# Beginning layer two's feed-forward with the first token tile while the second tile's residual is summed

## The chip, the cores and the metric

The kernel runs on one core of one Trainium2 chip. The metric is the device time of one execution in microseconds (us), the median of several runs. The engines are named as in the profile: PE (TensorE, matmul), DVE (VectorE), ACT (ScalarE), POOL (GpSimd), SP (SyncE, here only a queue of DMAs). "ps" tiles lie in PSUM, all others on chip in SBUF.

## The reference, cut to what matters

Two decoder layers on 256 tokens of width 2048 (two token tiles of 128). What the change touches is the seam between the second layer's output projection and its gated MLP:

```python
def _finish_layer(x, heads, w_o, norms, w_up, w_conv, b_conv, w_down):
    x = x + _rmsnorm(heads @ w_o, norms[1])
    f = _conv_ffn(_rmsnorm(x, norms[2]), w_up, w_conv, b_conv, w_down)
    return x + _rmsnorm(f, norms[3])

def _conv_ffn(h, w_up, w_conv, b_conv, w_down):
    u = h @ w_up
    gate, val = jnp.split(u, 2, axis=-1)
    ...
    return (jax.nn.silu(acc) * val) @ w_down
```

## The kernel before, in words

All products are made of float32 values split in two parts, a rounded high part (written by ACT) and the rest as a low part (written by DVE): high x high, low x high and high x low make three matmuls (`mm3`). Every weight goes by DMA into a `raw` tile (3 buffers) and is split into a `w` tile (4 buffers) by `split` (lines 699 and 700): a cast on ACT, a subtraction on DVE.

`out_proj` multiplies the attention heads by `wo_b` in four chunks of 512 columns. The last two pieces of the last chunk ("late") are held split in a tile of their own (`stores`), so that all products of token tile 0 come first and then those of tile 1. `evac` squares a finished bank with an accumulated sum (`square_into`, L270, ACT), makes the reciprocal root mean square (`rstd`: a sum on DVE, L262, a power on POOL, L264) and multiplies by the gain (L616, DVE). `add_normed` (L599, DVE) adds four chunks of 512 columns to the residual `x[:, t]`. For layer two the first tile's residual is summed while PE multiplies the second tile's products; the second's follows, and with each chunk of it `x_T` is called.

`x_T` turns the residual: PE transposes (L306) 128x128 blocks of both token tiles into a PSUM bank that holds two blocks of 256 columns. `scaled_T` scales each block by the norm's gain and splits it into `h`: high part by ACT (L294), low part by DVE (L295), each from the same bank. PSUM has two sets of four banks, tags "g" and "s".

`ffn` multiplies h by the up weights, first eight narrow tiles of 128 output columns (`narrow(0)`, `ws_pair`, `ws_tile`: 16 depth blocks `kt` of two matmuls each, L173, one of 512 columns and one of 256), and then in the wide phases (`wide`) by 512 columns at a time with seven products for every unit u of two depth blocks, the first three of them plain: product 1 and 2 with the first token tile's h. `first_sums` and `sums_of_h` prepare sums of weights and of h for the other four. `rms` (ACT squares of x, L270) gives the norm's factor, which is applied later.

What sets the order: the program is written for a scheduler that lays out each engine's queue from priorities, tile buffers and dependencies; instructions that pass through `pin` while `self.pinned` is set keep the order in which they are written. `later` and `step` put a piece of work behind a number of weight tiles. The scheduler also adds all waits on semaphores; two engines that read one PSUM bank are made to wait for each other.

Of the kernel before, what the change touches and what calls it, by code (L numbers as in the profile page):

```python
# [10 lines left out]
F32 = mybir.dt.float32  # L11
# [38 lines left out]
class Body:  # L50
# [59 lines left out]
    def piece(self, src, cuts=1, store=None, between=None):  # L110
# [13 lines left out]
        for h in range(2):  # L124
            if store:
                hi, lo = (v[:, h * 1024:(h + 1) * 1024] for v in store)
            else:
                hi, lo = self.halves()
# [28 lines left out]
    def ws_tile(self, out, src, h, fresh=False):  # L157


        b = self.bank()  # L160
        self.step()
        raw = self.sb.tile([P, 2048], F32, name="raw", tag="raw", bufs=3)
        self.nc.sync.dma_start(raw, src)
        parts = [self.ws_parts(raw, i, FAR if fresh else APART, fresh) for i in range(2)]
# [51 lines left out]
    def as_mm(self, banks, parts, lhs, pi, tiles=(0, 1), cols=slice(0, 512)):  # L216
# [7 lines left out]
        for k, t in order:  # L224
# [4 lines left out]
            self.mm3(banks[t][:, cols], hi[:, ts], lo[:, ts], whi[:, ks], wlo[:, ks], kt == 0, kt == n - 1)  # L229

# [14 lines left out]
    def stores(self, which):  # L245

        w = self.sb.tile([P, 4, 2048], F32R, name=which, tag=which, bufs=1)
        return [(w[:, 2 * i, :], w[:, 2 * i + 1, :]) for i in range(2)]
# [9 lines left out]
    def rstd(self, ss):  # L258
# [3 lines left out]
        nc.vector.reduce_sum(v, ss, axis=AX.X)  # L262
# [5 lines left out]
    def square_into(self, src, acc):  # L268
        junk = self.sb.tile([P, 512], BF16, name="junk", tag="junk", bufs=1)
        return self.nc.scalar.activation(junk[:, :src.shape[-1]], src, AF.Square, scale=float(D) ** -0.5, accum_out=acc)  # L270
# [18 lines left out]
    def scaled_T(self, src, kt, g, h):  # L289
# [4 lines left out]
        self.last_hi = nc.scalar.activation(hi[:, kt, :], src, AF.Copy, scale=gc)  # L294
        nc.vector.scalar_tensor_tensor(lo[:, kt, :], src, gc, hi[:, kt, :].bitcast(F32),  # L295
                                       op0=ALU.mult, op1=ALU.subtract)
# [296 lines left out]
    def add_normed(self, ys, r, t, each=None):  # L593

        for c in range(4):
            if each and c:
                each(c - 1)
            xs = self.x[:, t, c * 512:(c + 1) * 512]
            self.nc.vector.scalar_tensor_tensor(xs, ys[c][:, t, :], r, xs, op0=ALU.mult, op1=ALU.add)  # L599
# [3 lines left out]
    def out_proj(self, layer, src, lhs, each, filler=None):  # L603
# [3 lines left out]
        for c0 in (0, 2):  # L607
# [3 lines left out]
            def evac(i, t):  # L611
# [4 lines left out]
                nc.vector.tensor_tensor(ys[c][:, t, :], banks[i][t], gs[i], op=ALU.mult)  # L616
# [15 lines left out]
            if late:  # L632

                store = self.stores("h2")
                parts = [self.piece(src[c0 + i][pi], store=st) for (i, pi), st in zip(late, store)]
                for t in range(2):
                    for (i, pi), p in zip(late, parts):
                        self.as_mm(banks[i], p, lhs, pi, (t,))
                    evac(late[-1][0], t)
        if filler:  # L640
            self.later(3, lambda: self.add_normed(ys, r[1], 1, each))
            filler()
        else:
            self.add_normed(ys, r[1], 1, each)
# [66 lines left out]
    def wide(self, src, then, ahead, h, s, forms, r, beside, also, outs=None):  # L711
# [10 lines left out]
        ps = {i: self.bank("g" if i in (1, 2, 6, 7) else "s") for i in range(1, 8)}  # L722
# [12 lines left out]
        def copied(u):  # L735

            c = self.near[:, 16 + u % 2 * P:][:, :P]
            pin(nc.scalar.copy(c, lhs(1, u)[0]))
            return c

        def load(u):

            raw = self.sb.tile([P, 2048], F32, name="raw", tag="raw", bufs=3)
            pin(nc.sync.dma_start(raw[:, :1536], src[u][:, :1536]))
# [9 lines left out]
        def plain(raw):  # L754
            fa, fb = self.halves(), self.halves()
            self.split(*fa, raw[:, 0:1024])
# [21 lines left out]
        f, first = plain(raw), copied(0)  # L778
        self.pinned = True
        for u in range(n):  # L780
# [6 lines left out]
            product(1, u, fa, 1, first)  # L787
            product(2, u, fa, 0)
            product(3, u, fb, 0)
# [4 lines left out]
            if more:  # L794
                raw = load(u + 1)
                after = beside[u + 1]()
                t, f = sums(ahead.pop(0), raw), plain(raw)
# [42 lines left out]
    def ffn(self, layer, h, each, filler=None, done=None, late=None):  # L840
# [108 lines left out]
        def narrow(g):  # L949
            for p in (2 * g, 2 * g + 1):  # L950
# [3 lines left out]
                ga = self.ws_pair(up[w, 0], h)  # L954
# [56 lines left out]
        for g in WIDE:  # L1011
            phase = WIDE.index(g)
            then = uw[phase + 1] if g < WIDE[-1] else None
            made = self.wide(uw[phase], then, ahead, h, s, forms, R[0], beside(g + 1), rest if phase == 0 else {})
# [73 lines left out]
    def run(self):  # L1088
# [245 lines left out]
        hh, hl, _ = self.hset("h1")  # L1334
        heads[2] = (hh[:, 0:4, :], hl[:, 0:4, :])
        lhs = [(mh[:, i, :], ml[:, i, :]) for i in range(4)] + [outs(i) for i in range(12)]
        box = []

        def each(c):
            if not box:  # L1340
                box.append(self.hset("h2"))
            self.x_T(COL_G["b2"], box[0], [c])

        self.out_proj(1, a["wo_b"], lhs, each)
        h = box[0]

        def store(t, c):
# [3 lines left out]
        self.ffn(1, h, None, done=store)  # L1351
# [99 lines left out]
```

## Time and profile before

| | us |
|---|---|
| time, median of 3 runs | 2140.63 (2140.34 to 2140.84) |
| the profiled execution | 2141.77 |
| its span | 2139.9 |
| PE busy | 2126.7 (99%) |
| DVE busy | 1737.7 (81%) |
| ACT busy | 1360.5 (64%) |
| granted clock of PE | 0.999 |

The span reaches from the first to the last instruction; busy times leave out waits. In rows of the timeline the columns are start, duration, engine, line and operation, output and input, and a count where equal instructions follow each other without a break; in square brackets stands the idle time before the row and who ended it. L-numbers are lines of the kernel before.

### The profile page before, as it was taken

What the parts mean: (1) busy time and instruction counts of PE and PEld (TensorE: products, weight loads), DVE (VectorE), ACT (ScalarE), POOL (GpSimd) and SP (SyncE); (2) the same over time, 40 slices, a digit from 0 to 9 for tenths busy, and PEclk for the clock granted to TensorE, in tenths of its full rate; (3) what the DMA queues carried; (4) which work ended last, traced back from release to release, by engine and by line L of the source; (5) the groups of instructions that cost most, each with busy time, mean ns of one, the idle gap of its engine ahead of it and who ended that gap; (6) DMA issues with size and microseconds to landing.
All of it is one profiled execution on the core that took longest, in us unless ns stands there. A gap on an engine that the chain in (4) does not pass through costs nothing. (4 is left out here: it accounts for less than half of the span.)

```text
span 2139.9 us, 29276 instructions
## 1 busy us (share of the span) xinstructions
PE 2126.7 (99%) x10894; PEld 1814.7 (85%) x10894; DVE 1737.7 (81%) x2451; ACT 1360.5 (64%) x2101; POOL 178.5 (8%) x201
## 2 busy tenths in 40 slices
PE   9999999999999999999999999999999999999998
PEld 8888888888888888888888888878888888888887
DVE  7798867997887968778798977579978878787886
ACT  6667756676665666666685655466766656666663
POOL 0000001000101001010011000010101010110110
PEclk9999999999999999999999999999999999999999
DMA  9887557796979979798778745577979798897974
GB/s 356 263 267 256 177 177 266 226 280 231 297 237 284 283 216 303 237 282 264 281 270 264 267 160 175 189 239 228 290 219 298 237 286 271 245 299 223 295 249 184
DMA packets 111774, 538.82 MB, mean 252 GB/s; under 512 B 11280, under 2 KB 11664, under 8 KB 73488
## 3 DMA queue, kind: packets, MB, share of 16 engines
q1 hardware_dynamic: 75744, 445.66, 58.1%
q0 software_dynamic: 35744, 91.24, 21.3%
q8 instruction: 85, 1.39, 0.2%
q14 instruction: 57, 0.47, 0.1%
q10 hardware_dynamic: 144, 0.06, 0.0%
HBM read 510.17 MB, written 26.74 MB: 251 GB/s over the span
## 5 line engine op out<-in xcount | busy, mean ns | idle before, releaser
L700 DVE TENSOR_TENSOR w<-raw,w 128x1024 fp32r<-128x1024 f32 (+3 forms) x859 | 869.4, 1033 | 232.1 <-ACT w L699 231.1
L699 ACT CAST w<-raw 128x1024 fp32r<-128x1024 f32 (+3 forms) x859 | 752.6, 901 | 346.1 <-PE ps_g L143 164.5
L173 PE MATMUL ps_s<-h,w 128*128 128x256 f32 (+1 forms) x3200 | 577.6, 333 | 0.4 <-DVE w L700 0.3
L173 PEld LDWEIGHTS ps_s<-h,w 128*128 128x128 f32 x3200 | 496.5, 188 | 71.3 <-DVE w L700 1.0
L143 PE MATMUL ps_g<-w,sh 128*128 128x512 f32 x2232 | 517.3, 391 | 0.0
L143 PEld LDWEIGHTS ps_g<-w,sh 128*128 128x128 f32 x2232 | 417.0, 188 | 86.6 <-ACT sc L803 0.9
L173 PE MATMUL ps_g<-h,w 128*128 128x512 f32 (+1 forms) x1920 | 340.2, 336 | 0.8 <-DVE h L295 0.8
L173 PEld LDWEIGHTS ps_g<-h,w 128*128 128x128 f32 x1920 | 292.0, 188 | 39.0 <-DVE h L295 1.2
L143 PE MATMUL ps_g<-w,h 128*128 128x512 f32 x936 | 231.6, 390 | 0.4 <-ACT w L699 0.4
L700 DVE TENSOR_TENSOR x<-sh,x 128x1024 fp32r<-128x1024 f32 x192 | 227.1, 1220 | 0.2
L143 PEld LDWEIGHTS ps_g<-w,h 128*128 128x128 f32 x936 | 175.0, 188 | 34.5 <-DVE w L700 1.2
L699 ACT CAST x<-sh 128x1024 fp32r<-128x1024 f32 x192 | 193.6, 1052 | 0.9 <-DVE sh L751 0.8
L184 ACT COPY qk<-ps_s 128x256 f32<-128x256 f32 x96 | 35.8, 373 | 191.9 <-PE ps_s L173 191.9
L143 PE MATMUL ps_s<-x,h 128*128 128x512 f32 x552 | 155.0, 389 | 0.0
L707 POOL DMA_DIRECT2D sh<-in_uw_dram x80 | 98.4, 1229 | 647.7 <-DMA sh<-in_uw_dram 333.0
L143 PE MATMUL ps_g<-x,h 128*128 128x512 f32 x528 | 148.3, 389 | 0.0
L143 PEld LDWEIGHTS ps_s<-x,h 128*128 128x128 f32 x552 | 103.6, 188 | 21.5
L143 PEld LDWEIGHTS ps_g<-x,h 128*128 128x128 f32 x528 | 99.1, 188 | 17.1
L185 DVE TENSOR_TENSOR qk<-ps_s,qk 128x256 f32<-128x256 f32 x96 | 40.5, 422 | 69.8 <-ACT qk L184 69.8
L905 DVE SCALAR_TENSOR_TENSOR qk<-qk,cols 128x254 f32<-128x254 f32 (+1 forms) x176 | 80.3, 481 | 12.7 <-ACT qk L898 10.3
L143 PE MATMUL ps_s<-w,h 128*128 128x512 f32 x264 | 74.1, 389 | 0.0
L751 DVE TENSOR_TENSOR sh<-sh,raw 128x512 f32<-128x512 f32 x96 | 66.4, 692 | 3.2
(207 smaller groups left out, 1630.2 us busy)
## 6 DMA issues: line engine op xcount, KB each, us to landing
raw<-in_up_dram SPq DMA_DIRECT2D x96, 1024.0 KB, 7.1
raw<-in_dn_dram SPq DMA_DIRECT2D x88, 1024.0 KB, 5.3
raw<-in_uw_dram SPq DMA_DIRECT2D x80, 768.0 KB, 8.4
sh<-in_uw_dram SPq DMA_DIRECT2D x80, 512.0 KB, 8.8
sh<-in_uw_dram POOLq DMA_DIRECT2D x80, 512.0 KB, 10.6
raw<-in_wqk_a_dram SPq DMA_DIRECT2D x24, 1024.0 KB, 5.0
yout<-sh POOLq DMA_DIRECT2D x32, 512.0 KB, 7.5
raw<-in_wo_b_dram SPq DMA_DIRECT2D x16, 1024.0 KB, 4.8
```

The source lines that it names most:

```text
L143: mm = lambda *o, **k: self.pin(self.nc.tensor.matmul(*o, **k))
L173: mm = lambda *o, **kw: self.pin(self.nc.tensor.matmul(*o, **kw))
L184: self.pin(self.nc.scalar.copy(out, b[:, S:]))
L185: self.pin(self.nc.vector.tensor_add(out, b[:, 0:S], out))
L699: high = self.pin(self.nc.scalar.copy(hi, of))
L700: low = self.pin(self.nc.vector.tensor_sub(lo, of, hi.bitcast(F32)))
L707: self.nc.gpsimd.dma_start(d.rearrange("p (a n) -> p a n", a=2), src[u][:, 1536:].unsqueeze(1).to_broadcast([P, 2, 512]), accum_op=ALU.add)
L751: pin(add(half(e, 0), half(e, 1), half(raw, 0)))
L905: pin(nc.vector.scalar_tensor_tensor(c[:, j, d:], ga[:, j, :S - d], w[i], c[:, j, d:], op0=ALU.mult, op1=ALU.add))
```

## The change

The change alters the seam between `out_proj` and `ffn` of layer two only.

- While the second token tile's last products run, the first tile's residual is turned (`turned_x`, four blocks of one token tile in one bank) and scaled by itself (`scaled_x`, through `scaled_T` with 128 columns a block instead of 256). The second tile is turned and scaled after it in the same way.
- The weights of products 1 and 2 of the first two units of the first wide phase are loaded and split ahead (`early_weights`), and these 12 matmuls are made right after the second tile's (`early_products`), into the banks that the wide phase goes on with. The wide phase leaves them out (`skip`).
- The second tile's residual is added chunk by chunk (`add_chunk`) between scalings, and the first up tile's products (`tile(c)`, four depth blocks each) are written between these steps. The second up tile's first half of weights is split ahead too (`second`), the second half only behind the last scaling (`given`, `issue_after`).
- The late pieces are held in the free room of `h1` and one `w` tile instead of in `h2`, since h is now written into `h2` while they are still read.
- Order: from the first tile's evacuation on, squares, sums, residuals, transposes, scalings and products of this stage are pinned in the order in which they are written.

The diff, cut:

```diff
-    def ws_tile(self, out, src, h, fresh=False):
+    def ws_tile(self, out, src, h, fresh=False, given=None):
...
+        if given:
+            raw, part, (high, low) = given
+            with self.tc.issue_after(high.ins), self.tc.issue_after(low.ins):
+                parts = [part, self.ws_parts(raw, 1, APART, False)]
...
+            if k in behind:
+                behind[k]()
...
-        self.last_hi = nc.scalar.activation(hi[:, kt, :], src, AF.Copy, scale=gc)
-        nc.vector.scalar_tensor_tensor(lo[:, kt, :], src, gc, hi[:, kt, :].bitcast(F32),
-                                       op0=ALU.mult, op1=ALU.subtract)
+        self.last_hi = self.pin(nc.scalar.activation(hi[:, kt, ts], src, AF.Copy, scale=gc))
+        self.last_lo = self.pin(nc.vector.scalar_tensor_tensor(lo[:, kt, ts], src, gc, hi[:, kt, ts].bitcast(F32),
+                                                               op0=ALU.mult, op1=ALU.subtract))
...
+    def turned_x(self, t, c):
+
+        b = self.bank("s")
+        for k in range(4):
+            kt = c * 4 + k
+            self.pin(self.nc.tensor.transpose(b[:, k * P:(k + 1) * P], self.x[:, t, kt * P:(kt + 1) * P], self.ident))
+        return b
+
+    def scaled_x(self, t, c, b, g, h):
+        for k in range(4):
+            self.scaled_T(b[:, k * P:(k + 1) * P], c * 4 + k, g, h, slice(t * P, (t + 1) * P))
...
+    def early_weights(self, src):
+
+
+        raw = self.sb.tile([P, 2048], F32, name="raw", tag="raw", bufs=3)
+        for u in range(2):
+            self.nc.sync.dma_start(raw[:, u * 1024:(u + 1) * 1024], src[u][:, :1024])
+        hi, lo = self.halves()
+        self.split(hi, lo, raw[:, :1024])
...
+    def early_products(self, h, fs):
+
+        ps = [self.bank(), self.bank()]
+        for u, f in enumerate(fs):
+            for i in range(2):
+                lhi, llo = (h[2][:, 2 * u + i, a, 0:P] for a in range(2))
+                self.mm3(ps[i], lhi, llo, *f[i], u == 0, False)
+        return ps, len(fs)
...
+                banks[0] = None
+                begun = join[0]()
                 for t in range(2):
                     for (i, pi), p in zip(late, parts):
-                        self.as_mm(banks[i], p, lhs, pi, (t,))
+                        self.as_mm(banks[i], p, lhs, pi, (t,), behind=join[1](begun) if t and pi == n - 1 else {})
                     evac(late[-1][0], t)
+                    self.pinned = True
+                    if t == 0:
+                        join[2](begun)
+                banks[1] = None
...
+            join[3](begun, lambda c: self.add_chunk(ys, r[1], 1, c))
+            self.pinned = False
...
-            product(1, u, fa, 1, first)
-            product(2, u, fa, 0)
-            product(3, u, fb, 0)
+            if u < skip:
+                product(3, u, fb, 0, first)
+            else:
+                product(1, u, fa, 1, first)
+                product(2, u, fa, 0)
+                product(3, u, fb, 0)
...
+        def second(st):
+            st["raw"] = self.ws_load(up[1])
+            st["part"] = self.ws_parts(st["raw"], 0, APART, False)
+            st["h"] = self.hset("h2")
...
+        def among(st):
+            return {1: lambda: (turn(st, 0, 0), scale(st, 0, 0)), 2: lambda: turn(st, 0, 1)}
+
+        def finish(st, add):
+            h = st["h"]
+            for c in (2, 3):
+                turn(st, 0, c)
+            st["early"] = self.early_products(h, st.pop("fs"))
+            scale(st, 0, 1)
+            for c in range(2):
+                add(c)
+                turn(st, 1, c)
+            scale(st, 1, 0)
+            scale(st, 0, 2)
...
+            for c in range(2):
+                tile(c)
+                add(c + 2)
+                turn(st, 1, c + 2)
+                scale(st, 1, c + 1)
+                if not c:
+                    scale(st, 0, 3)
+            tile(2)
+            scale(st, 1, 3)
+            tile(3)
+            self.ws_sum(ga[:, 0, :], b)
```

ACT's queue of the kernel before, where h is scaled (names carry buffer numbers: `ps_s_12396` is one PSUM bank, `h2_12395` is h):

```order
L270 ACTIVATE junk_12387,sums_11768<-ps_g_12112 128x512 [waits PE_49,Activation_49]
L294 ACTIVATE h2_12395<-ps_s_12396,cols_63 128x256 [waits DVE_49,PE_49]
L738 COPY near_69<-h2_12395 128x128 [waits Activation_49]
L294 ACTIVATE h2_12395<-ps_s_12405,cols_63 128x256 [waits PE_49]
L294 ACTIVATE h2_12395<-ps_s_12415,cols_63 128x256 [waits PE_49]
L294 ACTIVATE h2_12395<-ps_s_12396,cols_63 128x256 [waits DVE_49]
L294 ACTIVATE h2_12395<-ps_s_12405,cols_63 128x256 [waits DVE_49]
L294 ACTIVATE h2_12395<-ps_s_12415,cols_63 128x256 [waits DVE_49]
```

The same place in the changed kernel (lines 278, 302 and 752 are the square, the scaling and the cast; h is `h2_12390`; `w_12387` is the second up tile's first half):

```order
L278 ACTIVATE junk_12374,sums_11768<-ps_g_12111 128x512 [waits PE_49]
L752 CAST w_12387<-raw_12385 128x1024 [waits DMAHW6_49,DVE_49,PE_49]
L302 ACTIVATE h2_12390<-ps_s_12409,cols_63 128x128 [waits PE_49]
L302 ACTIVATE h2_12390<-ps_s_12409,cols_63 128x128 [waits DVE_49] x3
L278 ACTIVATE junk_12433,sums_11768<-ps_g_12112 128x512 [waits PE_49,Activation_49]
L302 ACTIVATE h2_12390<-ps_s_12425,cols_63 128x128
L302 ACTIVATE h2_12390<-ps_s_12425,cols_63 128x128 [waits DVE_49] x3
L302 ACTIVATE h2_12390<-ps_s_12473,cols_63 128x128 [waits PE_49]
L302 ACTIVATE h2_12390<-ps_s_12473,cols_63 128x128 [waits DVE_49] x3
```

Four blocks of one bank now follow each other, and from the second on each waits for DVE; the second tile's square (`ps_g_12112`) stands behind the first four.

DVE's queue of the kernel before from the second tile's evacuation on:

```order
L262 TENSOR_REDUCE small_12389<-sums_11768 128x1 [waits Activation_49]
L616 TENSOR_TENSOR sh_11767<-ps_g_12112,sc_12115 128x512
L599 SCALAR_TENSOR_TENSOR x_10768<-sh_11764,small_12391,x_10768 128x512 [waits DMASW1_49,Pool_49]
L599 SCALAR_TENSOR_TENSOR x_10768<-sh_11765,small_12391,x_10768 128x512
L599 SCALAR_TENSOR_TENSOR x_10768<-sh_11766,small_12391,x_10768 128x512
L599 SCALAR_TENSOR_TENSOR x_10768<-sh_11767,small_12391,x_10768 128x512 [waits DVE_49]
```

The same in the changed kernel (L624 adds a residual chunk, L303 scales):

```order
L270 TENSOR_REDUCE small_12435<-sums_11768 128x1 [waits Activation_49]
L663 TENSOR_TENSOR sh_11767<-ps_g_12112,sc_12115 128x512
L303 SCALAR_TENSOR_TENSOR h2_12390<-ps_s_12425,cols_63,h2_12390 128x128 [waits PE_49,Activation_49]
L303 SCALAR_TENSOR_TENSOR h2_12390<-ps_s_12425,cols_63,h2_12390 128x128 [waits Activation_49] x3
L624 SCALAR_TENSOR_TENSOR x_10768<-sh_11764,small_12437,x_10768 128x512 [waits DMASW1_49,Pool_49]
L624 SCALAR_TENSOR_TENSOR x_10768<-sh_11765,small_12437,x_10768 128x512
L303 SCALAR_TENSOR_TENSOR h2_12390<-ps_s_12473,cols_63,h2_12390 128x128 [waits Activation_49] x4
L303 SCALAR_TENSOR_TENSOR h2_12390<-ps_s_12440,cols_63,h2_12390 128x128 [waits Activation_49] x4
L624 SCALAR_TENSOR_TENSOR x_10768<-sh_11766,small_12437,x_10768 128x512
L303 SCALAR_TENSOR_TENSOR h2_12390<-ps_s_12479,cols_63,h2_12390 128x128 [waits Activation_49] x4
L303 SCALAR_TENSOR_TENSOR h2_12390<-ps_s_12445,cols_63,h2_12390 128x128 [waits Activation_49] x4
L624 SCALAR_TENSOR_TENSOR x_10768<-sh_11767,small_12437,x_10768 128x512 [waits DVE_49]
```

The four residual chunks of the second tile no longer follow each other: four scalings come ahead of the first, and eight stand ahead of the third and of the fourth. On PE the changed kernel has the two up tiles' products (`ps_g_12500`, `ps_g_12590`) side by side between the transposes, and in front of the last of them a wait for a weight that is split last:

```order
L179 MATMUL ps_g_12500<-h2_12390,w_12347 128x512 [waits DVE_49]
L179 MATMUL ps_g_12500<-h2_12390,w_12347 128x256
L179 MATMUL ps_g_12590<-h2_12390,w_12617 128x512 [waits Activation_49]
L179 MATMUL ps_g_12655<-h2_12390,w_12667 128x512 [waits DVE_49,Activation_49]
L179 MATMUL ps_g_12590<-h2_12390,w_12617 128x256 [waits DVE_49]
```

Here `w_12617` is the second up tile's second half and `w_12667` the third's first: PE's product with the third tile stands ahead of the rest of the second.

More of the change, by code (lines that the diff above doesn't have):

```diff
@@ L124, in piece @@
         for h in range(2):
[L125 to L128, printed above, removed]
+            hi, lo = store[h] if store and store[h] else self.halves()
             for i in range(0, 1024, n):
@@ L214, in ws_pair, with as_mm @@
         return out
-    def as_mm(self, banks, parts, lhs, pi, tiles=(0, 1), cols=slice(0, 512)):
+    def as_mm(self, banks, parts, lhs, pi, tiles=(0, 1), cols=slice(0, 512), behind={}):
         n = len(lhs)
@@ L245, in stores @@
     def stores(self, which):
-        w = self.sb.tile([P, 4, 2048], F32R, name=which, tag=which, bufs=1)
-        return [(w[:, 2 * i, :], w[:, 2 * i + 1, :]) for i in range(2)]
+        w = self.sb.tile([P, 4, 2, 1024], F32R, name=which, tag=which, bufs=1)
+        return [[(w[:, 2 * i, h, :], w[:, 2 * i + 1, h, :]) for h in range(2)] for i in range(2)]
     def sums(self, n):
@@ L709, in first_sums, with wide @@
         return d
-    def wide(self, src, then, ahead, h, s, forms, r, beside, also, outs=None):
+    def wide(self, src, then, ahead, h, s, forms, r, beside, also, outs=None, early=None):
         nc, n = self.nc, KT // 2
-        ps = {i: self.bank("g" if i in (1, 2, 6, 7) else "s") for i in range(1, 8)}
+        given, skip = early if early else ((), 0)
+        ps = {i: given[i - 1] if i <= len(given) else self.bank("g" if i in (1, 2, 6, 7) else "s") for i in range(1, 8)}
         pin, add = self.pin, nc.vector.tensor_add
@@ L777, in wide @@
         next(b)
-        f, first = plain(raw), copied(0)
+        f, first = plain(0, raw), copied(0)
         self.pinned = True
@@ L796, in wide @@
                 after = beside[u + 1]()
-                t, f = sums(ahead.pop(0), raw), plain(raw)
+                t, f = sums(ahead.pop(0), raw), plain(u + 1, raw)
             self.catch_up()
@@ L838, in values, with ffn @@
         return V
-    def ffn(self, layer, h, each, filler=None, done=None, late=None):
+    def ffn(self, layer, h, each, filler=None, done=None, late=None, early=None, begun=None):
         nc = self.nc
@@ L1013, in ffn @@
             then = uw[phase + 1] if g < WIDE[-1] else None
-            made = self.wide(uw[phase], then, ahead, h, s, forms, R[0], beside(g + 1), rest if phase == 0 else {})
+            made = self.wide(uw[phase], then, ahead, h, s, forms, R[0], beside(g + 1), rest if phase == 0 else {},
+                             early=early if phase == 0 else None)
             for i in range(2):
@@ L1344, in run, with begin @@
[L1344 to L1347 removed]
+        up = a["up1"][0, 0]
+        def begin():
+            st = {"fs": self.early_weights(a["uw1"][0])}
+            raw = self.ws_load(up[0])
+            st["parts"] = [self.ws_parts(raw, i, APART, False)[0] for i in range(2)]
+            return st
+        def second(st):
+            st["raw"] = self.ws_load(up[1])
+            st["part"] = self.ws_parts(st["raw"], 0, APART, False)
+            st["h"] = self.hset("h2")
@@ new lines, in turn, with scale, tile @@
+        def turn(st, t, c):
+            st[t, c] = self.turned_x(t, c)
+        def scale(st, t, c):
+            self.scaled_x(t, c, st.pop((t, c)), COL_G["b2"], st["h"])
+        def among(st):
[11 more added lines that the diff above has]
+            scale(st, 0, 2)
+            b, ga = self.bank(), self.pairtile()
+            def tile(c):
+                whi, wlo = st["parts"][c // 2]
+                for k in range(4):
+                    self.ws_mm(b, whi[c % 2 * 4 + k], wlo[c % 2 * 4 + k], 0, h, 4 * c + k)
+            for c in range(2):
[9 more added lines that the diff above has]
+            self.ws_sum(ga[:, 0, :], b)
+            st["ga"] = ga, (st["raw"], st["part"], (self.last_hi, self.last_lo))
+            box.append(st)
@@ L1348, in store, with put @@
+        box = []
+        self.out_proj(1, a["wo_b"], lhs, None, store=store, join=(begin, among, second, finish))
+        h, early, ga = (box[0][k] for k in ("h", "early", "ga"))
+        def put(t, c):
             cs = slice(c * 512, (c + 1) * 512)
             nc.sync.dma_start(a["out"][t][:, cs], self.x[:, t, cs])
-        self.ffn(1, h, None, done=store)
+        self.ffn(1, h, None, done=put, early=early, begun=ga)
 def _feature_tiles(w):
```

64 lines of the change are left out of this document (41 added, 23 removed).

## The prediction

> **What bounds the kernel now.** I read the page's busy times first, then the chain of waits of TensorE (PE), then the timeline of the stage that the change touches, engine by engine, then the costs grouped by form. The page, the busy time of two stretches (columns: stretch, its length; then busy time and count for PE, weight loads, VectorE (DVE), ScalarE (ACT), GpSimd; clock; DMA share; GB/s), and PE's own rows:
>
> ```profile
> span 2139.9 us, 29276 instructions
> PE 2126.7 (99%) x10894; PEld 1814.7 (85%) x10894; DVE 1737.7 (81%) x2451; ACT 1360.5 (64%) x2101; POOL 178.5 (8%) x201
> ...
> 1422.78:1450.19 27.41, 24.23 (x150) 21.07 (x149) 22.96 (x46) 21.90 (x48) 4.10 (x8) 1.00 0.66 192
> 1450.19:1470.00 19.81, 19.81 (x120) 17.62 (x119) 19.81 (x42) 14.39 (x23) 0.95 (x1) 1.00 0.52 174
> ...
> 1417.34 2.88 PE L143 MATMUL ps_g<-h,sh 128*128 128x512 f32 x12
> 1420.06 2.89 PE L143 MATMUL ps_g<-h,h 128*128 128x512 f32 x12
> 1422.78 0.60 PE L306 MATMUL ps_s<-ident,x 128*128 128x128 f32 x4
> 1425.41 1.54 PE L306 MATMUL ps_s<-ident,x 128*128 128x128 f32 x12 [2.03 <-DVE x L599]
> 1427.79 0.96 PE L173 MATMUL ps_g<-h,w 128*128 128x512 f32 x4 [0.85 <-DVE h L295]
> 1429.06 1.50 PE L306 MATMUL ps_s<-ident,x 128*128 128x128 f32 x12 [0.31 <-DVE h L295]
> 1430.32 1.62 PE L173 MATMUL ps_g<-h,w 128*128 128x512 f32 x8
> 1431.77 0.60 PE L306 MATMUL ps_s<-ident,x 128*128 128x128 f32 x4
> 1432.13 18.06 PE L173 MATMUL ps_g<-h,w 128*128 128x512 f32 x104
> ```
>
> PE is busy 99% of the span at a granted clock of 1.00, so the kernel ends when PE's work is done, and only PE's waits can be won or lost. In this stage they are 2.03 + 0.85 + 0.31 = 3.19 us. Work by rate: 12 products of 512 columns take 2.72 us (1417.34 to 1420.06), so 0.227 each; the 104 of line 173 take 0.172 each; 12 transposes take 1.26 (1429.06 to 1430.32), 0.105 each. The stretch from 1422.78 to 1450.19 holds 116 of line 173 and 32 transposes, 19.95 + 3.36 = 23.3 us of work in 27.4: 4.1 us are lost, the 3.19 and some refilling of the pipe. That is all that the change can win here, 0.19%. Behind it PE waits for nothing, while DVE is busy 19.81 of 19.81 us: it has no room to fall behind.
>
> What makes PE wait, from the rows of the other engines:
>
> ```profile
> 1417.53 0.60 ACT L270 ACTIVATE junk<-ps_g 128x512 bf16<-128x512 f32 x1 [4.39 <-PE ps_g L143]
> 1418.26 0.16 DVE L262 TENSOR_REDUCE small<-sums 128x1 f32<-128x6 f32 x1 [3.85 <-ACT junk L270]
> 1419.10 2.74 DVE L599 SCALAR_TENSOR_TENSOR x<-sh,small,x 128x512 f32<-128x512 f32 x4
> 1423.04 0.60 ACT L270 ACTIVATE junk<-ps_g 128x512 bf16<-128x512 f32 x1 [4.82 <-PE ps_g L143]
> 1423.76 0.16 DVE L262 TENSOR_REDUCE small<-sums 128x1 f32<-128x6 f32 x1 [1.92 <-ACT junk L270]
> 1424.60 2.74 DVE L599 SCALAR_TENSOR_TENSOR x<-sh,small,x 128x512 f32<-128x512 f32 x4
> 1427.26 4.29 DVE L295 SCALAR_TENSOR_TENSOR h<-ps_s,cols,h 128x256 fp32r<-128x256 f32 x10
> 1427.77 1.62 ACT L294 ACTIVATE h<-ps_s,cols 128x256 fp32r<-128x256 f32 x4 [0.23 <-DVE h L295]
> 1433.07 0.47 ACT L294 ACTIVATE h<-ps_s,cols 128x256 fp32r<-128x256 f32 x1 [0.18 <-DVE h L295]
> 1433.57 0.48 DVE L295 SCALAR_TENSOR_TENSOR h<-ps_s,cols,h 128x256 fp32r<-128x256 f32 x1 [0.15 <-ACT h L294]
> ```
>
> PE waits for the square, the sum and the residual of the second tile (1423.04 to 1425.35). Then h is scaled: ACT writes the high part of a column block, DVE reads the same PSUM block and writes the low part. The marks on ACT's rows matter most: ACT waits for DVE. In the built program its second read of a PSUM bank waits until DVE has read that bank's first block. Before, two blocks share a bank, and ACT takes the first of three banks before it returns, so the two engines overlap: ten of DVE's in 4.29 us, 0.43 each.
>
> **The change, step by step.** All 32 half-width scalings are pinned bank after bank, four blocks in each bank. ACT's block k+1 waits for DVE's block k, which waits for ACT's block k: they take turns. Prices:
>
> ```profile
> L294 ACT ACTIVATE h<-ps_s,cols 128x256 fp32r<-128x256 f32 x48 | 20.2, 489 | 4.1 <-PE ps_s L306 3.6 <-DVE h L295 0.4
> L184 ACT COPY qk<-ps_g 128x256 f32<-128x256 f32 x48 | 17.7, 368 | 35.0 <-PE ps_g L173 32.3 <-PE ps_s L525 2.4
> L738 ACT CAST near<-h 128x128 fp32r<-128x128 f32 x96 | 28.2, 294 | 0.0
> L295 DVE SCALAR_TENSOR_TENSOR h<-ps_s,cols,h 128x256 fp32r<-128x256 f32 x48 | 20.2, 478 | 1.4 <-ACT h L294 1.1
> L599 DVE SCALAR_TENSOR_TENSOR x<-sh,small,x 128x512 f32<-128x512 f32 x32 | 22.1, 746 | 1.6 <-POOL small L264 1.4
> L675 DVE SCALAR_TENSOR_TENSOR qk<-qk 128x128 f32<-128x128 f32 x48 | 13.7, 286 | 0.4
> ...
> 1433.44 1.05 ACT L699 CAST w<-raw 128x1024 fp32r<-128x1024 f32 x1
> 1434.52 1.23 DVE L700 TENSOR_TENSOR w<-raw,w 128x1024 fp32r<-128x1024 f32 x1 [0.46 <-ACT w L699]
> 1434.76 0.62 ACT L270 ACTIVATE junk<-x 128x512 bf16<-128x512 f32 x1
> 1435.28 0.19 ACT L270 ACTIVATION_READ_ACCUMULATOR junk<-x 128x1 f32 x1
> ```
>
> No row has a scaling of 128 columns. ACT: copies fall from 368 to 294 ns from 256 to 128 columns, so 489 becomes about 0.41 us; floor 0.30 (the cast), ceiling 0.49 (no saving). DVE: 478 at 256 and 746 at 512 give 134 per 128 columns, so 0.34; floor 0.286, ceiling 0.48. A hand-over takes 0.03 (ACT's 1433.07 + 0.47, DVE's 1433.57). I take the middle values, since the same operation lies nearest. A turn is 0.41 + 0.03 + 0.34 + 0.03 = 0.81 us, and a bank 4 x 0.75 + 7 x 0.03 = 3.2.
>
> [...]
>
> In the clock of before:
> - Work moved, not added: 12 products (2.7 us) from the wide phase, and their weights' splits. The transfers and GpSimd's queue:
>
> ```profile
> 1401.02 13.74 SPq L163 DMA_DIRECT2D raw<-in_up_dram  x5
> 1403.24 1.22 DVE L700 TENSOR_TENSOR w<-raw,w 128x1024 fp32r<-128x1024 f32 x1
> 1404.37 2.35 DVE L700 TENSOR_TENSOR h<-raw,h 128x1024 fp32r<-128x1024 f32 x2
> 1414.86 0.85 SPq L706 DMA_DIRECT2D sh<-in_uw_dram  x2
> 1421.84 1.26 POOL L707 DMA_DIRECT2D sh<-in_uw_dram  x1 [2.78 <-DMA sh<-in_uw_dram]
> ...
> DMA to landing us min/median/max: 4.9/5.0/5.7
> ```
>
>   The uw pair goes onto SP ahead of up, into the buffer that DVE leaves at 1404.4 (up's first was issued at 1401.02), and lands near 1409.5. The two up tiles follow in the buffers left at 1406.7 and, after the late half's split, 1408, and land by 1413. Their splits (1.05 + 2 x 0.6 on ACT for the uw pair, where the second up tile took 2.1) end near 1414, ahead of 4.39 us of idle ACT and 3.85 of DVE: 0, and with 3 us less cover the square at 1417.53 would be late. GpSimd's power for the second tile stands behind an accumulation that waits for uw's sh transfer. That one is issued about 1 us later than at 1414.86, so GpSimd is free by 1424.1, ahead of the sum: 0. In the wide phase two transfers become two pairs, and PE never waits there for SP: 0.
> - First tile: PE puts 8 transposes into the second tile's 24 products (to 1423.6), 8 more (1424.5), 12 early products (1427.2). DVE is done with the first residual at 1421.84, splits one more half of up weights (1.23), and takes turns with ACT on the first bank from 1423.07 to 1425.8. That is ahead of PE: 0.
> - Second residual: its square now stands behind those four turns on ACT, at 1425.4 instead of 1423.04, and on DVE another bank of the first tile (1426.1 to 1429.7) stands ahead of the first residual chunk. It ends at 1430.4, before at 1425.35. PE stands from 1427.2 to 1430.4: 3.26.
> - Then two banks stand between residual chunks on DVE, 6.0 us; the third chunk starts at 1437.0 and the fourth at 1443.2. PE has meanwhile 4 transposes and 16 products of both up tiles, 3.2 us, and waits 0.24 + 0.73 + 2.80 + 0.21 + 2.80.
> - The last 8 blocks give PE one tile's 0.34 us each against turns of 0.81: 1.24 + 1.42. The last block is done at 1449.4.
> - Only then ACT splits the second half of the second up tile, behind a square (0.74 + 1.05): 1.03. The next product in PE's order is already the third tile's and waits for a copy, a square and a cast more: 1.94. In before two whole tiles were split ahead.
>
> Waits in after: 3.26 + 0.24 + 0.73 + 2.80 + 0.21 + 2.80 + 1.24 + 1.42 + 1.03 + 1.94 = 15.7 us, against 4.1: 11.6 more. With the floors the same walk gives 7.1, with the ceilings 17.7. Behind it DVE has two more halves to split than before at the same point of PE's work, 2.4 us, mostly in room that PE's delay has made; 0 to 2.4, I take 0.5, since DVE's queue comes out about 1 us ahead of PE at the wide phase. Sum 12.1. The profiled run took 2141.77 us (span 2139.9, 1.9 around it), so 2153.9 on that scale; it lies 1.1 above the median of 2140.63, and on the median's scale it is 2152.7.
>
> **Rivals.**
> 1. The turns don't bind: ACT and DVE overlap over banks as in the 4.29 us row. For it speaks that row; against it the waits in the built order, and the two marks of 0.23 and 0.18. Walked with the same prices without that wait, PE's loss is 4.0 (the tail's 2.7 stays): 2140.5, floors 2139.3. This is the case on the other side, not slower; it decides once ACT's next block can start before DVE's is done, a turn of about 0.4.
>    [...]
> 2. All waits are covered and the tail too, because the next up tile's split finds ACT free: 2140.6 - 4.1 = 2136.5. Against it: that split is issued behind the last scaling.
> 3. The turns bind and DVE stays behind in the saturated stretch: the ceilings or 2.4 more, 2155 to 2160.
>
> **How the numbers follow.** A change of 0.2% (4.3 us) is about what a measurement tells from none. The turns bind, with 3 as its upper end: 0.82, at 2147.7 to 2160. Rival 1: 0.13. Rival 2: 0.05, of which 0.03 is beyond 0.2%. So slower 0.81 (a little of the first case may fall short), within 0.2% 0.15, faster 0.04. Of the first case nearly all lies above 2146; to leave out no more than 0.2 the range is 2145 to 2160.
>
> **What would show it.** ACT and DVE alternate in single rows with marks on each other from 1422 to 1450; scaling rows near 0.41 and 0.34; transposes that wait three times some 3 us for the residual; the second residual's last chunk 15 us or more later; PE's waits for w behind it. It is wrong if ACT's scaling rows merge into groups of four, if PE's idle time in the stage stays under 5 us, or if the wide phase gives back what the stage lost.

## The result and the profile after

The changed kernel takes 2153.74 us (median of four runs, 2153.4 to 2156.05) against 2140.49 for the kernel before on the same chip: 13.25 us more, a ratio of 1.0064 with a 95% interval of 1.0047 to 1.0082. The forecast was 2152.7, slower, in a range of 2145 to 2160. Run again later, the changed kernel gave 2153.91 against 2141.16. The first profile of it was taken in its slowest run (2156.05).

The page's first lines after the change (span; then busy time of the engines):

```profile
span 2154.3 us, 29315 instructions
...
PE 2135.1 (99%) x10894; PEld 1818.0 (84%) x10894; DVE 1741.5 (81%) x2468; ACT 1364.8 (63%) x2118; POOL 178.7 (8%) x201
```

PE's busy time has grown by 8.4 us, though it does the same 10894 matmuls. Part of that is products that take longer, as the rows of PE show further down: 16 of them fill 4.58 us where 0.172 each would be 2.75. Both timelines meet at the first tile's square (1417.53 in both). ACT and DVE in the stage of the change (L302 and L303 scale, L278 squares, L624 adds a residual chunk):

```profile
1417.53 0.60 ACT L278 ACTIVATE junk<-ps_g 128x512 bf16<-128x512 f32 x1 [2.94 <-PE ps_g L140]
...
1425.10 0.59 ACT L278 ACTIVATE junk<-ps_g 128x512 bf16<-128x512 f32 x1
1426.86 0.37 ACT L302 ACTIVATE h<-ps_s,cols 128x128 fp32r<-128x128 f32 x1 [0.82 <-DVE h L303]
1427.65 0.37 ACT L302 ACTIVATE h<-ps_s,cols 128x128 fp32r<-128x128 f32 x1 [0.42 <-DVE h L303]
...
1427.26 0.35 DVE L303 SCALAR_TENSOR_TENSOR h<-ps_s,cols,h 128x128 fp32r<-128x128 f32 x1 [0.43 <-ACT h L302]
1428.05 0.35 DVE L303 SCALAR_TENSOR_TENSOR h<-ps_s,cols,h 128x128 fp32r<-128x128 f32 x1 [0.43 <-ACT h L302]
...
1429.10 1.41 DVE L624 SCALAR_TENSOR_TENSOR x<-sh,small,x 128x512 f32<-128x512 f32 x2
1436.24 0.74 DVE L624 SCALAR_TENSOR_TENSOR x<-sh,small,x 128x512 f32<-128x512 f32 x1
1442.14 0.74 DVE L624 SCALAR_TENSOR_TENSOR x<-sh,small,x 128x512 f32<-128x512 f32 x1
1447.77 0.35 DVE L303 SCALAR_TENSOR_TENSOR h<-ps_s,cols,h 128x128 fp32r<-128x128 f32 x1 [0.44 <-ACT h L302]
```

ACT and DVE alternate in single rows, each marked with the other: one block in 0.785 us (1426.86 to 1427.65 is 0.79), while each works for 0.37 and 0.35. The residual chunks stand between these turns, and the last block is done at 1448.1. PE in the same stage:

```profile
1425.94 1.56 PE L140 MATMUL ps_g<-qk,h 128*128 128x512 f32 x6
1429.90 1.32 PE L336 MATMUL ps_s<-ident,x 128*128 128x128 f32 x8 [2.40 <-DVE x L624]
1431.40 4.58 PE L179 MATMUL ps_g<-h,w 128*128 128x512 f32 x16 [0.18 <-DVE h L303]
1437.04 0.66 PE L336 MATMUL ps_s<-ident,x 128*128 128x128 f32 x4 [1.06 <-DVE x L624]
1437.45 3.18 PE L179 MATMUL ps_g<-h,w 128*128 128x512 f32 x16
1442.93 0.66 PE L336 MATMUL ps_s<-ident,x 128*128 128x128 f32 x4 [2.31 <-DVE x L624]
...
1449.33 0.50 PE L179 MATMUL ps_g<-h,w 128*128 128x512 f32 x1 [0.43 <-ACT w L752]
1451.16 4.07 PE L179 MATMUL ps_g<-h,w 128*128 128x512 f32 x13 [1.33 <-DVE w L753]
```

Three waits for the residual ahead of transposes (L336), then two for weights that are split late, ahead of products of the up tiles (L179). Sixteen products that take 2.75 us at 0.172 each fill 4.58 us at 1431.40; in the profile of the later run (the second profile), with the clock at 1.00 there, they fill 3.32. The granted clock in the first profile (columns: stretch, length, PE busy, clock, DMA, GB/s):

```profile
1424.00:1431.40 7.40, 4.82 (x28) 1.00 0.86 201
1431.40:1434.80 3.40, 3.40 (x11) 0.50 0.57 102
...
1445.20:1448.40 3.20, 3.20 (x11) 0.50 0.49 205
1448.40:1451.80 3.40, 1.64 (x7) 1.00 0.00 0
1451.80:1455.20 3.40, 3.40 (x12) 0.51 0.92 306
1455.20:1470.00 14.80, 14.80 (x89) 1.00 0.62 214
```

Three times, right behind a stretch in which PE stood a good part of the time, the clock is half for about 3.4 us. In the first two stretches ACT and DVE set the pace anyway: from the transposes at 1429.90 to those at 1437.04 it is 7.14 us, from those at 1442.93 to the late weight at 1449.33 it is 6.40, and both are the same in the second profile, which has the clock at 1.00 in the one and at half in an earlier part of the other. In the third PE is the bound and loses half of 3.4, that is 1.7 us: the 79 products from 1451.16 on fill 15.47 us, and 13.66 in the second profile, at 1.00.

PE's last products start 13.98 us later than before (2142.66 against 2128.68; the spans differ by 14.4). Where these 13.98 us arise is read from the first product of the wide phase and of its third unit (operand `near`), before and then after:

```profile
1477.08 0.40 PE L143 MATMUL ps_g<-w,near 128*128 128x512 f32 x1
...
1497.71 0.39 PE L143 MATMUL ps_g<-w,near 128*128 128x512 f32 x1
```

```profile
1491.92 0.40 PE L140 MATMUL ps_s<-w,near 128*128 128x512 f32 x1
...
1493.20 0.50 PE L140 MATMUL ps_s<-w,h 128*128 128x512 f32 x1 [0.65 <-DVE w L753]
...
1511.47 0.40 PE L140 MATMUL ps_g<-w,near 128*128 128x512 f32 x1
```

The first is 14.84 us later with 12 products (2.72 us) already done: 12.1 us lost in the stage. The third unit's is 13.76 later, with all 12 used up: 1.6 more, of which 0.65 + 0.23 stand in PE's rows as waits for `w`. The last 0.2 is lost in the two units behind it; from the fifth unit's first product to the end the distance stays at 13.98.

### The profile page after: what moved, and what is told of

Same layout as the page of the kernel before. It is cut to its first block, busy times and chain, and to the rows that moved or that the text cites. A ratio compares the mean times of both kernels' runs of the same rounds, so it can differ in the third digit from the quotient of the medians.

```text
span 2154.3 us, 29315 instructions
## 1 busy us (share of the span) xinstructions
PE 2135.1 (99%) x10894; PEld 1818.0 (84%) x10894; DVE 1741.5 (81%) x2468; ACT 1364.8 (63%) x2118; POOL 178.7 (8%) x201
## 5 line engine op out<-in xcount | busy, mean ns | idle before, releaser
L179 PE MATMUL ps_s<-h,w 128*128 128x256 f32 (+1 forms) x3200 | 578.9, 333 | 1.0 <-DVE w L753 0.9
L179 PEld LDWEIGHTS ps_s<-h,w 128*128 128x128 f32 x3200 | 496.8, 188 | 72.9 <-DVE w L753 2.0
L179 PE MATMUL ps_g<-h,w 128*128 128x512 f32 (+1 forms) x1920 | 347.5, 340 | 2.2 <-DVE w L753 1.3
L179 PEld LDWEIGHTS ps_g<-h,w 128*128 128x128 f32 x1920 | 296.2, 190 | 43.3 <-ACT w L752 2.4
L191 DVE TENSOR_TENSOR qk<-ps_s,qk 128x256 f32<-128x256 f32 x96 | 40.5, 421 | 68.9 <-ACT qk L190 68.9
L967 DVE SCALAR_TENSOR_TENSOR qk<-qk,cols 128x254 f32<-128x254 f32 (+1 forms) x176 | 80.3, 481 | 12.7 <-ACT qk L960 10.3
```

The source lines that it names most:

```text
L179: mm = lambda *o, **kw: self.pin(self.nc.tensor.matmul(*o, **kw))
L191: self.pin(self.nc.vector.tensor_add(out, b[:, 0:S], out))
L967: pin(nc.vector.scalar_tensor_tensor(c[:, j, d:], ga[:, j, :S - d], w[i], c[:, j, d:], op0=ALU.mult, op1=ALU.add))
```

## Experiments

Theory T is the prediction's: turns of ACT and DVE over one PSUM bank set when h is done. The table has the medians; "last block" and "wide phase" are the end of the last scaling and the start of the wide phase's first product, counted from the first tile's square in the same profile (kernels without the early products have 2.7 us more to do behind that point). Line numbers in their rows are those of the edited kernels.

| kernel | us | before, same chip | ratio (95%) | last block | wide phase |
|---|---|---|---|---|---|
| before | | | | | 59.6 |
| changed | 2153.74 | 2140.49 | 1.0047 to 1.0082 | 30.6 | 74.4 |
| changed, again | 2153.91 | 2141.16 | 1.0049 to 1.0076 | 30.6 | 72.6 |
| e1 pairs | 2148.24 | 2141.79 | 1.0021 to 1.0048 | 25.1 | 68.9 |
| e2 residual first | 2154.68 | 2141.79 | 1.0042 to 1.0076 | 30.0 | 74.9 |
| e3 no early products | 2158.20 | 2141.79 | 1.0063 to 1.0093 | 31.1 | 74.5 |
| e4 early second half | 2153.75 | 2141.79 | 1.0041 to 1.0071 | 33.2 | 72.8 |
| e5 all repairs | 2142.83 | 2141.01 | 0.9999 to 1.0017 | 21.3 | 61.8 |
| e6 first pair | 2146.49 | 2141.01 | 1.0015 to 1.0036 | 22.3 | 65.7 |
| e7 blocks dealt | 2150.37 | 2141.01 | 1.0028 to 1.0059 | 26.8 | 69.9 |
| e8 before, bank after bank | 2146.91 | 2141.01 | 1.0019 to 1.0041 | | 66.6 |
| e9 repairs, DVE relieved | 2141.38 | 2141.34 | 0.9994 to 1.0012 | 21.3 | 62.2 |
| e10 before, DVE relieved | 2141.57 | 2141.34 | 0.9995 to 1.0012 | | 59.5 |
| e11 kept busy | 2153.36 | 2141.16 | 1.0044 to 1.0069 | | 72.5 |

**e1, pairs.**

```diff
-            scale(st, 1, 0)
-            scale(st, 0, 2)
+            two(st, (1, 0), (0, 2))
...
-                scale(st, 1, c + 1)
-                if not c:
-                    scale(st, 0, 3)
+                two(st, *(((1, 1), (0, 3)), ((1, 2), (1, 3)))[c])
...
-            scale(st, 1, 3)
```

`two` scales block k of one bank, then block k of the other.

> The changed kernel with one edit: the six banks that are scaled behind the second tile's first two residual chunks are scaled two banks at a time, block by block in turn (bank A block 0, bank B block 0, A block 1 ...). Every instruction, PE's order and the place of every residual chunk stay. Theory (turns over one PSUM bank): ACT's next block no longer waits for DVE's last, two blocks come out in the 0.785 us that one took, and eight blocks take about 3.4 us instead of 5.6; the third residual chunk moves from 1436.2 to about 1433.7 and the last scaling from 1448.1 to about 1443. Time about 2148.5 (2147 to 2150). Rival A (the blocks are half as wide, so there are twice as many instructions with a fixed price each): the number stays, so the time stays at 2153.7. Rival B (only the place of the residual chunks in the queue counts, not the turns): no change of more than 1 us, 2153 to 2154.

It took 2148.24: 6.5 us above before where the changed kernel has 12.8 to 13.3. ACT's rows, two blocks each now:

```profile
1430.02 0.63 ACT L302 ACTIVATE h<-ps_s,cols 128x128 fp32r<-128x128 f32 x2 [0.16 <-DVE h L303]
1430.80 0.63 ACT L302 ACTIVATE h<-ps_s,cols 128x128 fp32r<-128x128 f32 x2 [0.16 <-DVE h L303]
```

Two blocks come out in 0.78 us, the time that one took, and the last block is 5.5 us earlier. Number and width of the blocks (rival A) are unchanged, so they are not what these 6.3 to 6.8 us are.

**e7, blocks dealt over two banks.** Only where the transposes write is edited:

```diff
+        if t or c > 1:
+            if c % 2 == 0:
+                self.dealt = self.bank("s"), self.bank("s")
+            bs = [self.dealt[k % 2][:, (c % 2 * 2 + k // 2) * P:][:, :P] for k in range(4)]
```

> The changed kernel with one edit, in the transposes alone: the four blocks of a chunk are dealt over two PSUM banks, and two neighbouring chunks share these two banks (chunks 2 and 3 of the first tile, all chunks of the second; each bank still holds four blocks). The order of scalings, residual chunks and products is word for word that of the changed kernel. Theory (ACT's next read of a bank waits for DVE's read of the same bank): neighbours in the order now lie in different banks, two blocks come out in each 0.785 us, the last scaling ends near 1442 instead of 1448.1; one pair of banks comes free later and costs PE up to 2.6 us ahead of the second tile's third chunk: 2148 to 2151. Rival A (number and width of the blocks) and any theory in which the order alone matters: 2153.7.

2150.37, as expected, though the last block is done 2.3 us later than expected (26.8 in the table, 24.5). The last chunks' transposes stand behind products on PE, and 20 of these take 5.85 us where 0.172 each would be 3.4: the clock in this profile is half from 1428.4 to 1435.2. The order on ACT and DVE is that of the changed kernel, and yet four blocks follow each other:

```profile
1430.59 1.14 ACT L302 ACTIVATE h<-ps_s,cols 128x128 fp32r<-128x128 f32 x4 [0.16 <-DVE h L303]
1431.90 1.15 ACT L302 ACTIVATE h<-ps_s,cols 128x128 fp32r<-128x128 f32 x4 [0.16 <-DVE h L303]
```

So the wait belongs to the PSUM bank, not to the order of the blocks. Whether the chip itself needs it, or only the schedule that adds the semaphore, no run tells: the wait alone was not taken away.

**e2, residual first; e4, second half early.** In e2 `add(c)` for all four chunks stands behind `scale(st, 0, 1)` and ahead of the other scalings. In e4 the second half of the second up tile is split ahead of the third bank (`st["part2"] = self.ws_parts(st["raw"], 1, APART, False)`, without `issue_after`).

> The changed kernel with one edit: all four residual chunks of the second tile are added one after the other at 1429.1, ahead of the six banks that stood between them; the turns stay. Theory (turns set the end): the six banks take their turns 1.3 us later and end where they ended, near 1448; PE waits for h instead of for the residual; 2153.7, within 1.5 of it. Rival B (PE's waits for the residual, 1.06 + 2.31 us by the trace, are lost because of where the chunks stand): these waits go and are not replaced, 2150 to 2151.

> The changed kernel with one edit: the second half of the second up tile is split ahead of the third scaled bank instead of behind the last scaling; the scheduler then also puts the third tile's two halves among the scalings of the fifth and sixth bank. Theory (ACT and DVE take turns and set the end): three splits of about 1.2 us come into the turns, h is done up to 3.7 us later, and the tail's waits for w (0.43 + 1.33) and the wide phase's (0.65 + 0.23) go: within 2 us of 2153.7. Rival D (the late split and the backlog behind it are a loss of their own): 2150 to 2151.

2154.68 and 2153.75: both as T has it. Neither the place of the residual nor the late split is a loss of its own while the turns last. The waits only move, in e2 from the residual to h, in e4 from the tail to the residual's last chunk, ahead of which splits now stand on DVE (one row of PE from each):

```profile
1441.23 0.61 PE L179 MATMUL ps_g<-h,w 128*128 128x512 f32 x2 [1.48 <-DVE h L303]
```

```profile
1443.71 1.12 PE L335 MATMUL ps_s<-ident,x 128*128 128x128 f32 x4 [4.37 <-DVE x L623]
```

**e3, no early products.** `early_weights` and `early_products` are left out, `early` is None.

> The changed kernel without the early products: their weights are not loaded and split ahead, and the 12 products stay in the wide phase. The rest stays. Theory: they only filled a stretch in which PE had to stand (2.40 us of it were left), so PE stands 2.7 us longer there and does the 12 products later; the wide phase's waits for w of 0.65 and 0.23 us may go, so 2154.7 to 2156.5. Rival C (the early weights' transfers and splits are what costs): the time falls by 1 us or more.

2158.20, 16.4 above before: 3.2 to 3.7 more than the changed kernel, so the early products earn what they move. The expectation was 1 to 2.8 more. PE stands 2.9 us longer ahead of the first transposes (5.26 against 2.40), as expected, and behind it the mean clock of a stretch is 0.68; half-rate time, which I had not counted, is the likely rest (an estimate from this row):

```profile
1428.80 1.97 PE L336 MATMUL ps_s<-ident,x 128*128 128x128 f32 x8 [5.26 <-DVE x L624]
```

```profile
1428.80:1436.40 7.60, 6.33 (x24) 0.68 0.29 48
```

**e8, the kernel before, bank after bank.** Its scalings of 256 columns are pinned in the order of their banks (`self.pin` in `scaled_T`, `self.pinned` around `x_T`).

> The kernel before with one edit: layer two's scalings, 256 columns wide and two blocks in a bank as ever, are pinned in the order in which they are written, so that a bank's two blocks follow each other. Theory: the second block of each bank waits for DVE, as in the changed kernel; a bank takes about 1.5 us instead of 0.87, the last of the 16 blocks is done near 1439 instead of 1434, and PE, which needs 0.69 us for what one block gives it, loses little against 0.75 a block: 1 to 4 us slower than before. If the wait belongs to blocks of 128 columns, or to the early products, no change.

It is 5.9 us slower, more than the 1 to 4 expected. A bank takes 1.42 us (ACT's starts), and the bill comes later, when DVE, held up 0.54 us per bank, is late with a weight (the last three rows show the clock there, in the columns used above):

```profile
1427.20 0.84 ACT L294 ACTIVATE h<-ps_s,cols 128x256 fp32r<-128x256 f32 x2 [0.58 <-DVE h L295]
1428.62 0.84 ACT L294 ACTIVATE h<-ps_s,cols 128x256 fp32r<-128x256 f32 x2 [0.58 <-DVE h L295]
...
1427.70 0.88 DVE L295 SCALAR_TENSOR_TENSOR h<-ps_s,cols,h 128x256 fp32r<-128x256 f32 x2 [0.54 <-ACT h L294]
...
1466.14 13.41 PE L173 MATMUL ps_g<-h,w 128*128 128x256 f32 x62 [3.13 <-DVE w L700]
...
1465.00:1466.00 1.00, 0.00 (x0) 0.50 0.00 0
1470.00:1471.00 1.00, 1.00 (x5) 0.50 0.57 82
1472.00:1473.00 1.00, 1.00 (x7) 1.00 1.11 459
```

The wait of 3.13 us is not all. From within it to 1471.8 the clock is half, and the 62 products behind it take 13.41 us where 0.172 each would be 10.7: up to 2.7 us more, which the expectation had left out. The turn, with two blocks a bank, full width and no edit but the pinned order, makes the kernel before slower; in this profile a good part of the price comes by the clock.

**e6 and e5, the repairs.** e6 is e1 with the first two banks as a pair ahead of the square: `{1: lambda: (turn(st, 0, 0), turn(st, 0, 1), two(st, (0, 0), (0, 1)))}`. e5 goes on from there (its diff is against the changed kernel):

```diff
             for c in range(2):
                 add(c)
                 turn(st, 1, c)
-            scale(st, 1, 0)
-            scale(st, 0, 2)
+            two(st, (1, 0), (1, 1), (0, 2), (0, 3))
...
+            tile(0, 4, 1, 5, 2, 6)
+            for c in (2, 3):
+                add(c)
+                turn(st, 1, c)
+            tile(3, 7)
+            st["part2"] = self.ws_parts(st["raw"], 1, APART, False)
+            two(st, (1, 2), (1, 3))
+            tile(8, 12, 9, 13, 10, 14, 11, 15)
```

> The version with pairs, and one edit more: the first tile's first two banks are turned one after the other and scaled block by block in turn, ahead of the second tile's square; no bank stands between that square and the second tile's residual any more. Theory: the first residual chunk then waits for the square, the sum and GpSimd's power alone and starts at about 1427.5 instead of 1429.1, PE's wait of 2.41 us ahead of it falls to about 1, and all that follows moves up as much: 1 to 2.2 us less than with the pairs alone (2148.24), 2146 to 2147.3. If the residual's start is set by the square and by GpSimd anyway, no change.

> A version made from the theory, to see whether the idea can beat both kernels: the first two banks of the first tile are scaled block by block in turn and ahead of the second tile's square; then two residual chunks, four banks in turn (16 blocks at 0.27 us each instead of 0.785), two chunks, the split of the second half of the second up tile, and the last two banks in turn; the first up tile's products follow the order in which h comes; the third tile's splits stand behind the last scaling. Theory: the last scaling is done near 1440 (1448.1 in the changed kernel), PE waits under 1 us for the residual and 1 to 2 us for h; by PE's work done it is then up to 1.5 us ahead of the kernel before, less 0 to 1.9 us of DVE's backlog behind it: 2139 to 2143, about the time before. If something other than the turns holds the changed kernel back, it stays above 2147.

e6 took 2146.49 and e5 2142.83, both in the forecast; e5 regains some 11 of the 13 us. In e6 PE's wait ahead of the first residual chunks falls from 2.41 to 0.24, further than the forecast of about 1. e5's rows on DVE and PE:

```profile
1429.00 3.97 DVE L309 SCALAR_TENSOR_TENSOR h<-ps_s,cols,h 128x128 fp32r<-128x128 f32 x15 [0.31 <-ACT h L308]
```

```profile
1427.24 1.32 PE L342 MATMUL ps_s<-ident,x 128*128 128x128 f32 x8 [0.26 <-DVE x L630]
...
1434.11 1.03 PE L342 MATMUL ps_s<-ident,x 128*128 128x128 f32 x8
...
1480.36 0.50 PE L140 MATMUL ps_s<-w,h 128*128 128x512 f32 x1 [0.92 <-DVE w L759]
```

With four banks in turn a block costs 0.265 us (3.97 for 15), and PE waits 0.26 for the first residual chunks and not at all for the last. It starts the wide phase 2.2 us after the kernel before (61.8 against 59.6) with 2.7 us of it done, 0.5 ahead, and then loses 1.8 up to the third unit, of which 0.92 + 0.29 stand as waits for `w`.

**e9 and e10, DVE relieved.** `nc.gpsimd.tensor_add` instead of `nc.vector.tensor_add` for the first addition of `sums_of_h` in the first five units, in e5 and in the kernel before.

> The version with all repairs, and one edit more: of the sums of h that the wide phase needs, the first addition (128x512, 0.68 us each on DVE) of the first few units runs on GpSimd instead of DVE, three of them ahead of the norm's power there. If what is left of the loss (PE's waits for w of 0.92 and 0.29 us at the start of the wide phase) is DVE's backlog, 2 us less work on DVE takes 1 to 1.8 us off: 2141 to 2142 where the version without it took 2142.83, about the time before. If these waits come from the order of PE's products or from the transfers, no change; if GpSimd is much slower than DVE at it, its power and DVE's next additions come late and the time rises.

> The kernel before with the same edit alone: the first additions of the first units' sums of h on GpSimd. PE does not wait for DVE in this stretch, so by either theory the time stays, within 1 us of the kernel before. If it falls, the relief is worth something by itself, and no part of it belongs to the change.

2141.38 and 2141.57, against 2141.34 for the kernel before. e9's wait of 0.92 at the start of the wide phase is gone, but PE meets another earlier:

```profile
1464.35 11.34 PE L185 MATMUL ps_g<-h,w 128*128 128x512 f32 x64 [1.52 <-DVE qk L197]
```

e9 is level with before; no version beats both. That its gain over e5 is real is not shown, since their intervals overlap.

**e11, PE kept busy.**

```diff
+            if half and given:
+                both = h[2][:, KT - 1, :, :].rearrange("p a t -> p (a t)")
+                for k in range(8):
+                    self.nc.tensor.matmul(b, self.zero, both, start=False, stop=False)
```

> The changed kernel with one edit: eight matmuls with a weight tile of zeros, 512 columns each, are put on PE right behind the last scaling, where PE stands for the weights that are split last (0.43 and 1.33 us); they add zero to the second up tile's sum. All other queues stay word for word. In the changed kernel's trace the granted clock is 0.5 in three stretches of 3.4 us, each behind a stretch in which PE stood: 1431.4 to 1434.8, 1445.2 to 1448.4 and 1451.8 to 1455.3; only in the last is PE itself the bound. If the clock follows PE's idleness, the last stretch is gone (clock 1.00 from 1451 on) and the time falls by about 1.7 us, half of 3.4. If the clock is lowered by something else, the eight matmuls change nothing that can be measured, or cost up to 0.5 us.

> The changed kernel itself, unedited, on the same chip as the run beside it, so that a difference of a microsecond can be told: 2153.7 by its first runs.

2153.36 against 2153.91 beside it: the 1.7 us did not show. The clock of e11 (first) and of the changed kernel's second profile, taken in a run of 2152.63:

```profile
1424.00:1450.40 26.40, 18.08 (x85) 1.00 0.38 96
1450.40:1470.00 19.60, 19.59 (x116) 1.00 0.69 229
```

```profile
1441.20:1444.70 3.50, 3.50 (x13) 0.51 0.62 262
1444.70:1449.40 4.70, 2.54 (x11) 1.00 0.07 28
1449.40:1460.00 10.60, 10.60 (x62) 1.00 0.75 247
```

With the filling the clock stays at 1.00, but it does so ahead of the filling too (the eight products start at 1447.87), behind waits of 2.40, 2.33 and 2.32 us like those of the unedited kernel. And the unedited kernel, with the same waits, here has one half-rate stretch instead of three, and none where PE is the bound. So the stretches are not in every execution, and that the filling kept the clock up is not shown; what it can save is at most 1.7 us in some executions, and these runs don't resolve it.

## Why the prediction was right, point by point

- **The turns bind:** shown by e1 (same instructions, other order) and e7 (same order, other banks), and from the other side by e8. Rival 1, with which it would have been 2140.5, is refuted; its decisive point, a turn of about 0.4, is what e1 makes. The time it was given does not hold either: e6, where all banks go in pairs at about 0.39 us a block, still took 2146.49. Where that walk went wrong stays open.
- **Size of a turn:** 0.785 us against 0.81. ACT's block took 0.37 (0.41 taken), DVE's 0.35 (0.34), and each hand-over 0.03 to 0.04.
- **Two banks between residual chunks:** 6.0 us forecast. ACT's first block of the next bank did not wait (at 1432.95 two of its blocks follow each other without a break), and two banks took 5.65 (1430.59 to 1436.24). The square came at 1425.10 (1425.4), the first chunk at 1429.10 (1429.7), the third at 1436.24 (1437.0), the fourth at 1442.14 (1443.2), the last block ended at 1448.1 (1449.4).
- **PE's waits:** forecast 3.26, 2.80 and 2.80 for the residual and 1.03 and 1.94 for weights. The traces have 2.40, 1.06 (2.32 in the second profile, where the clock was 1.00 in that stretch), 2.31, 0.43 and 1.33. All smaller, because the turns are shorter and because part of a wait lies inside rows of products that trickle (16 in 3.18 us at 1437.45, where 0.172 each would be 2.75). Counted by progress the stage lost 10.3 us in the second profile, and 12.1 in the first, against 11.6.
- **A term that the prediction lacked:** the clock. I took it as 1.00 throughout, from a profile that had no half-rate stretch in this part. Behind waits of this length (1.33 to 2.40 us) the changed kernel's first profile has three half-rate stretches of some 3.4 us (clock 0.50 to 0.51), and its second has one (3.5 us at 0.51, from 1441.2); where PE is the bound, in the last of the first profile, it is 1.7 us: nearly the whole difference between 10.3 and 12.1.
- **A term mis-sized:** "downstream DVE backlog", 0 to 2.4, of which I took 0.5. It measured 1.6 in the first profile and 1.7 in the second (from the wide phase's first product to its third unit), in the upper half. The reason I gave, that DVE's queue comes out 1 us ahead of PE, does not hold: PE's rows there wait for DVE's `w`, 0.65 + 0.23 us in the first profile and 0.85 + 0.30 in the second.
- **Sum:** 10.32 + 1.74 + 0.31 = 12.4 in an execution without the third half-rate stretch, 12.12 + 1.64 + 0.22 = 14.0 in one with it; medians 12.8 and 13.3; forecast 12.1. That the forecast lies so close is partly luck: the stage was put at 11.6 where it lost 10.3 with no half-rate stretch at its end, and this made up for a backlog put 1.1 to 1.2 too low and, in part, for the missing clock.
- **The rest costed at nothing** (early products' transfers and splits, GpSimd's queue, the first tile's part) held: the first tile's square stands at 1417.53 in the first profile of each kernel, in the others between 1415.5 and 1417.0 whatever the edit, and e3 shows that the early products gain.
- **Rival 2** (all hidden, 2136.5) was far off: even with all repairs it ends level. Of the 4.1 us to be won, the narrow blocks probably take back some (no run tells it apart): 32 on DVE at 0.265 are 8.5 us where 16 at 0.43 are 6.9, on an engine without room. Breaking the scalings up brought nothing here: 2153.7 with neighbours in one bank, 2142.8 with all repairs, 2141.0 before, and in the kernel before DVE behind this stage was busy 19.81 of 19.81 us.

## What to carry to other kernels

Before you cut an operation of two engines into smaller ones, look at which PSUM bank neighbours in the order lie in, and deal them over two or more, or alternate between two: here that alone gave back 3.4 to 3.9 us (e7) and 6.3 to 6.8 (e1) of 13. This kernel, with PE busy 99% of the span, had 4.1 us to win in this stage, and DVE, busy 19.81 of 19.81 us behind it before the change, had no room to take work late: up to the wide phase's third unit 1.6 to 1.8 us were lost (changed kernel, e5), of which 0.9 to 1.2 stand as waits for DVE's `w`. Where a change makes PE wait for microseconds, add the clock: here up to half of 3.4 us behind a stretch of waits, in e8 half of nearly 7, and not in each execution.

## What was not expected of the hardware

The granted clock fell to half (0.50) for about 3.4 us, in some profiles twice that (6.8 us in e7 and e8), even where PE had stood only 2 to 3 us (2.03 and 3.13 in e8), and in the same kernel three times in one profile and once in another. Behind the 2.03 us wait that the kernel before has in this stage, e8's profile has the clock at half from 1424.0 to 1427.4, the profile of the kernel before nowhere here. What exactly brings it down is not shown: the profiles of e5, e6 and e9, whose waits in this stage are at most 1.52 us, have no such stretch, but that of e11, with waits up to 2.40, has none either. An addition of 128x512 that takes DVE 0.68 us took GpSimd from 1.30 us to 3.34 in the rows of e9:

```profile
1444.81 1.30 POOL L742 TENSOR_TENSOR qk<-h 128x512 f32<-128x512 f32 x1 [7.85 <-DVE h L357]
...
1461.68 3.34 POOL L742 TENSOR_TENSOR qk<-h 128x512 f32<-128x512 f32 x1 [7.09 <-DVE qk L736]
```
